# Output projection of each 256 token block from seven half products

## The chip, the cores and the metric

One core of a Trainium2 chip runs the whole program. The metric is the device time of one execution in microseconds. Its engines are TensorE (matmuls; PE in the profile, PEld for its weight loads), VectorE (DVE), ScalarE (ACT), GpSimd (POOL) and SyncE (SP, which issues most DMAs). Each works off a queue of its own in order.

## The reference

One layer of a hybrid encoder on 2048 tokens of width 1024, with 16 meta tokens ahead. After an RMSNorm one input projection feeds two mixers, causal pooling (512 channels) and latent attention (4 heads of 128). Both are gated; then

```
mix = concat([pool_out, attn_out], axis=-1) @ w_out      # 2048 x 1024 @ 1024 x 1024
h   = h + mix
out = rmsnorm(h, final_norm_g)[:, 16:]
```

All inputs and outputs are float32.

## The kernel before

The kernel keeps float32 accuracy with float16 matmuls: a value is scaled by a power of two and split in a high and a low float16 part, and a product takes three matmuls (high x high, high x low, low x high) into one float32 sum.

The first 450 us hold the token projection and the attention. What follows is a list, TAIL (line 66), of short words that the program emits in order. `w`, `a0` to `a3`, `f`, `b` load, fold, scale and split the columns of w_in; `x3` to `x7` load and split the normalised input of a block of 256 tokens; a word of two digits such as `34` is `pair(3, 4)`: for block 3, two groups of 128 columns (each 24 matmuls of 256 columns, line 633), with the windows' sums (line 648), means (653) and gates (660 to 665) on ScalarE, VectorE and GpSimd. `o0` to `o7` load a slab of 128 rows of w_out and take the maximum of its magnitude (line 685), `s` makes the scale from it (`scale_wo`), `v0` to `v7` split a slab (`split_wo`). `p0` to `p15` prepare a tile of 128 tokens for the output projection (`op_prep`: scale and split the mixers' values, lines 747 and 748, and load the residual), and `q0` to `q15` do it (`op`).

`op` of a tile makes two halves of 512 columns. Each is 8 slabs x 3 = 24 matmuls of 512 columns into one bank (line 765); VectorE then adds the scaled sum to the residual (line 767) and ScalarE squares it (769). The last tile has one half of 512 and two pieces of 256 (LASTP). Then come the norm and the store.

The order inside a queue is the compiler's: it walks the list with a model of the engines, and an engine takes the earliest word of the list whose inputs are ready in the model. So an engine's order follows TAIL loosely; TensorE's order is fixed at compile time. TensorE writes to eight banks, six of them (tag "s", NS) for the pairs and the projection. Two pools hold two buffers each for the raw loads (`raw`), taken in turn.

Of the kernel before, what the change touches and what calls it, by code (L numbers as in the profile page):

```python
# [91 lines left out]
def hymba(tc, hT, hcat, tab, w_tok, w_m, w_out, wqT, wqr, wkT, wv, pool_w,  # L92
          gains, gkv, gfin, out):
    nc = tc.nc
# [580 lines left out]

    def load_wo(k):
        if k == 0:
            cw["wor"] = cpools[1].tile([P, KT, D], F32, name="wor")
            cw["wo"] = cpools[1].tile([P, 2, KT, D], F16, name="wo")
# [1 line left out]
        wr = cw["wor"][:, k]
        nc.sync.dma_start(out=wr, in_=w_out[:, k])
        for n in range(2):
            junk = cw["pool"].tile([P, 512], F16, name=f"woa{k}_{n}", tag="wa", bufs=1)
            nc.scalar.activation(out=junk, in_=wr[:, n * 512:n * 512 + 512], func=AF.Abs, accum_out=cw["womx"][:, 2 * k + n:2 * k + n + 1])

    def scale_of(name, cols, t, up):
        nc.vector.reduce_max(out=t[:, 0:1], in_=cols, axis=AX.X)
        spread_max(nc, bank("m", name), t, 1, 1, ident, t[:, 1:2])
        power_scale(nc, t[:, 1:2], t[:, 2:3], t[:, 3:4], up)  # L690
        return t[:, 2:3], t[:, 3:4]

    def scale_wo():
# [1 line left out]
        cw["oinv"], cw["osc"] = scale_of("womx", w[:, 0:16], w[:, 16:20], WSC)

    def split_wo(k):
        wr, wo, sc = cw["wor"], cw["wo"], cw["osc"]
        a, b = slice(0, 512), slice(512, 1024)
        nc.scalar.mul(out=wo[:, 0, k, a], in_=wr[:, k, a], mul=sc)  # L700
        nc.vector.scalar_tensor_tensor(out=wo[:, 1, k, a], in0=wr[:, k, a], scalar=sc, in1=wo[:, 0, k, a], op0=ALU.mult, op1=ALU.subtract)
        nc.scalar.mul(out=wr[:, k, b], in_=wr[:, k, b], mul=sc)
        nc.scalar.copy(out=wo[:, 0, k, b], in_=wr[:, k, b])
        nc.gpsimd.tensor_tensor(out=wo[:, 1, k, b], in0=wr[:, k, b], in1=wo[:, 0, k, b], op=ALU.subtract)
# [28 lines left out]
    mhl = {}

    def op_prep(t):
        if t == 0:
            cw["mh"] = cw["pool"].tile([P, 2, 2, KT, P], F16, name="mh", tag="x0", bufs=1, padded_shape=[P, 2, 2, KT, 136])
        mh, ml = cw["mh"][:, t % 2, 0], cw["mh"][:, t % 2, 1]
        w = mmx[t // 2]
        if t % 2 == 0:  # L740
            inv, sc = scale_of(f"mmx{t}", w[:, 0:4], w[:, 4:8], WSC)
            nc.vector.tensor_scalar(out=w[:, 8:9], in0=inv, scalar1=cw["oinv"], scalar2=float(2.0 ** (-2 * WSC)), op0=ALU.mult, op1=ALU.mult)
        sc = w[:, 7:8]
        a = attn[t // 2][:, :, (t % 2) * P:(t % 2 + 1) * P]
        m = mixg[t // 2][:, :, (t % 2) * P:(t % 2 + 1) * P]
        for o, x in ((0, m), (4, a)):
            nc.scalar.mul(out=mh[:, o:o + 4], in_=x, mul=sc)
            nc.vector.scalar_tensor_tensor(out=ml[:, o:o + 4], in0=x, scalar=sc, in1=mh[:, o:o + 4], op0=ALU.mult, op1=ALU.subtract)
# [4 lines left out]
    def op(t):
        mh, ml, xr = mhl.pop(t)
        gf = cw["gf"]
        ss = cpools[1].tile([P, 6], F32, name=f"oss{t}", tag="oss", bufs=3)
        pieces = ((0, 512), (512, 512)) if t < SEQ // P - 1 else LASTP
        for hf, (c0, w) in enumerate(pieces):
            ps = bank("s", f"op{t}_{hf}")
            sl = slice(c0, c0 + w)  # L760
            i = 0
            for k in range(KT):
                wh, wl = cw["wo"][:, 0, k], cw["wo"][:, 1, k]
                for (x, y) in ((mh, wh), (mh, wl), (ml, wh)):
                    nc.tensor.matmul(ps[:, :w], lhsT=x[:, k], rhs=y[:, sl], start=i == 0, stop=i == 3 * KT - 1)  # L765
                    i += 1
            nc.vector.scalar_tensor_tensor(out=xr[:, sl], in0=ps[:, :w], scalar=mmx[t // 2][:, 8:9], in1=xr[:, sl], op0=ALU.mult, op1=ALU.add)  # L767
            sq = cw["pool"].tile([P, 512], F16, name=f"osq{t}_{hf}", tag="wa", bufs=1)
            nc.scalar.activation(out=sq[:, :w], in_=xr[:, sl], func=AF.Square, scale=1.0 / 32.0, accum_out=ss[:, hf:hf + 1])  # L769
        nc.vector.reduce_sum(out=ss[:, 4:5], in_=ss[:, 0:len(pieces)], axis=AX.X)  # L770
# [166 lines left out]
```

## Time and profile before

| | us |
|---|---|
| median of 3 runs | 890.15 (888.6 to 891.38) |
| the profiled execution | 889.79 |
| its span, first to last instruction | 888.0 |
| TensorE busy | 848.8 |
| VectorE busy | 536.8 |
| ScalarE busy | 480.6 |
| GpSimd busy | 321.3 |

The span is the profiled execution's own; 1.8 us of its time lie outside. Busy time is the union of an engine's instructions: matmuls overlap, so the sum of their durations is more than their busy time. A row of a group gives busy time and the mean of one instruction; a row of the timeline gives start, length and how many instructions are merged in it.

### The profile page before, as it was taken

How to read it: one execution, taken by the hardware profiler on the slowest of the kernel's cores; microseconds unless marked ns; L12 is line 12 of the kernel's file. 1: busy time of each engine (PE TensorE's matmuls, PEld its weight loads, DVE VectorE, ACT ScalarE, POOL GpSimd, SP SyncE). 2: the span in 40 equal slices, each digit the busy share in tenths (PEclk: the TensorE clock that was granted, in tenths of full speed). 3: DMA queues.
4: the chain of work that ended last, by engine and by line, in shares of the span. 5: the costliest groups of instructions: out<-in, count | busy, mean ns of one | idle time of the engine just before them, and what ended most of it. 6: DMA issues, size and time to landing. Idle time of an engine off the chain costs nothing. (4 is left out here: it accounts for less than half of the span.)

```text
span 888.0 us, 16286 instructions
## 1 busy us (share of the span) xinstructions
PE 848.8 (96%) x5835; PEld 684.0 (77%) x5835; DVE 536.8 (60%) x1268; ACT 480.6 (54%) x1268; POOL 321.3 (36%) x512
## 2 busy tenths in 40 slices
PE   9979989999999999898888998999999999999996
PEld 8969968889888888787877897866666666667644
DVE  6657769856757667878624578775455344435242
ACT  6656756757777667785634684854242332232321
POOL 2666642434545453645313124641141121111100
PEclk9989999999999999998999999999999999999998
DMA  8755525977798788884786112212133122111111
GB/s 287 219 170 161 163 46 100 175 145 136 131 148 150 137 153 155 168 156 130 147 180 247 48 55 76 75 26 76 48 90 107 48 72 72 48 49 48 48 40 56
DMA packets 206956, 101.80 MB, mean 115 GB/s; under 512 B 169257, under 2 KB 196363, under 8 KB 206875
## 3 DMA queue, kind: packets, MB, share of 16 engines
q1 hardware_dynamic: 187392, 93.30, 44.0%
q10 hardware_dynamic: 19483, 7.47, 3.7%
q8 instruction: 46, 0.75, 0.4%
q14 instruction: 35, 0.29, 0.1%
HBM read 55.60 MB, written 8.43 MB: 72 GB/s over the span
## 5 line engine op out<-in xcount | busy, mean ns | idle before, releaser
L633 PEld LDWEIGHTS <-w 128*128 128x128 f16 x2304 | 226.8, 99 | 36.7 <-ACT w L617 2.3
L633 PE MATMUL mp<-xx,w 128*128 128x256 f16 x2016 | 229.4, 275 | 0.6 <-DVE gt L662 0.6
L765 PE MATMUL op<-wo,mh 128*128 128x512 f16 (+1 forms) x792 | 168.1, 373 | 0.0
L765 PEld LDWEIGHTS <-mh 128*128 128x128 f16 x792 | 77.5, 98 | 85.5
L472 POOL TENSOR_TENSOR hl<-p,hl 128x512 f16<-128x512 f32 (+4 forms) x104 | 105.0, 1031 | 94.9 <-ACT hl L470 94.8
L467 ACT ACTIVATE p<-s,st 128x512 f32<-128x512 f32 (+8 forms) x168 | 99.4, 600 | 63.2 <-DVE st L452 53.0
L446 DVE TENSOR_REDUCE st<-s 128x1 f32<-128x512 f32 (+6 forms) x154 | 88.7, 589 | 19.0 <-PE s L444 17.5
L503 PE MATMUL o<-pt,vh 128*128 128x256 f16 x544 | 92.2, 274 | 2.3 <-DMA pt<-hl 2.3
L470 ACT CAST hl<-p 128x512 f16<-128x512 f32 (+6 forms) x168 | 82.5, 541 | 4.1 <-DMA pt<-hl 3.9
L769 ACT ACTIVATE osq<-xr 128x512 f16<-128x512 f32 (+1 forms) x33 | 20.4, 617 | 100.0 <-DVE xr L767 78.0
L503 PE MATMUL o<-pt,vl 128*128 128x256 f16 x272 | 74.4, 274 | 0.0
L660 ACT ACTIVATE th<-mp,whalf 128x256 f32<-128x256 f32 x64 | 30.0, 469 | 72.6 <-PE mp L633 58.7
L767 DVE SCALAR_TENSOR_TENSOR xr<-op,mmx,xr 128x512 f32<-128x512 f32 (+1 forms) x33 | 24.2, 734 | 72.4 <-PE op L765 72.4
L503 PEld LDWEIGHTS <-vh 128*128 128x128 f16 x544 | 52.1, 98 | 11.6 <-issue 2.6
L771 POOL TENSOR_SCALAR oss<-oss 128x1 f32<-128x1 f32 x16 | 3.9, 246 | 154.6 <-DVE oss L770 154.6
L472 DVE TENSOR_TENSOR hl<-p,hl 128x512 f16<-128x512 f32 (+7 forms) x64 | 50.6, 792 | 8.1 <-ACT hl L470 7.5
L440 PE MATMUL s<-klo,qh 128*128 128x512 f32 (+9 forms) x116 | 46.2, 398 | 8.5 <-ACT p L467 5.4
L573 DVE SCALAR_TENSOR_TENSOR yr<-yr,gxs,rbc 128x256 f32<-128x256 f32 (+1 forms) x64 | 35.5, 617 | 15.8 <-DMA yr<-hT_in 15.7
L441 PE MATMUL s<-klo,qh 128*128 128x512 f32 (+9 forms) x116 | 43.5, 375 | 0.0
L442 PE MATMUL s<-klo,ql 128*128 128x512 f32 (+9 forms) x116 | 43.5, 375 | 0.0
L444 PE MATMUL s<-klo,qr 128*128 128x512 f32 (+9 forms) x116 | 43.2, 373 | 0.0
L577 POOL TENSOR_TENSOR xx<-yr,xx 128x512 f16<-128x512 f32 x28 | 36.0, 1299 | 19.8 <-ACT xx L576 19.8
(229 smaller groups left out, 1756.6 us busy)
## 6 DMA issues: line engine op xcount, KB each, us to landing
xt<-hcat_in SPq DMA_DIRECT2D x16, 512.0 KB, 6.7
xr<-hcat_in SPq DMA_DIRECT2D x16, 512.0 KB, 3.8
raw<-hT_in SPq DMA_DIRECT2D x15, 512.0 KB, 5.0
out_dram<-xr SPq DMA_DIRECT2D x15, 512.0 KB, 2.7
yr<-hT_in SPq DMA_DIRECT2D x14, 512.0 KB, 3.8
wr<-w_m_in SPq DMA_DIRECT2D x12, 512.0 KB, 4.2
rb<-rd ACTq DMA_DIRECT2D x32, 128.0 KB, 4.6
wor<-w_out_in SPq DMA_DIRECT2D x8, 512.0 KB, 6.5
```

The source lines that it names most:

```text
L440: nc.tensor.matmul(ps[:, :w], lhsT=q(qh), rhs=kt[:, 0, 0, sl], start=True, stop=False)
L441: nc.tensor.matmul(ps[:, :w], lhsT=q(qh), rhs=kt[:, 1, 0, sl], start=False, stop=False)
L442: nc.tensor.matmul(ps[:, :w], lhsT=q(ql), rhs=kt[:, 0, 0, sl], start=False, stop=False)
L444: nc.tensor.matmul(ps[:, :w], lhsT=q(qr), rhs=kt[:, 1, 1, sl], start=False, stop=True)
L446: nc.vector.reduce_max(out=mx[:, bi:bi + 1], in_=ps[:, :w], axis=AX.X)
L467: nc.scalar.activation(out=pr[:, o:o + w], in_=pss[bi][:, :w], func=AF.Exp, bias=nb_, accum_out=sm[:, bi:bi + 1] if nb > 1 else tot)
L470: nc.scalar.copy(out=hl[:, 0, sl], in_=pr[:, sl])
L472: eng.tensor_tensor(out=hl[:, 1, sl], in0=pr[:, sl], in1=hl[:, 0, sl], op=ALU.subtract)
L503: nc.tensor.matmul(ps[:, :2 * P], lhsT=v, rhs=x, start=i == 0, stop=i == len(ops) - 1)
L577: nc.gpsimd.tensor_tensor(out=xl[:, k:k + 2], in0=xr[:, k - k0:k - k0 + 2], in1=xh[:, k:k + 2], op=ALU.subtract)
L633: nc.tensor.matmul(ps[:, :n - sk], lhsT=a[:, k], rhs=x[:, k, sk:n], start=e == 0, stop=e == 3 * KT - 1)
L765: nc.tensor.matmul(ps[:, :w], lhsT=x[:, k], rhs=y[:, sl], start=i == 0, stop=i == 3 * KT - 1)
```

## The change

A block of 256 tokens is a matrix of two halves of rows (its two tiles, A1. and A2.) and two halves of columns (pooling and attention, A.1 and A.2); w_out is cut in quarters in the same way. The four half products of the block, each a sum of two products of quarters, eight in all, are made from seven products of sums and differences of the quarters (Strassen's method in Winograd's form). The sums are made in float32 and then split in float16 pairs.

For w_out four sums are made for each slab pair (t1 to t4), and seven matrices are split in place of four; `split_wo(n)` works on slab pair n // 2, an even n making the sums and three of the splits, an odd n the other four. For a block, `op_prep` of the even tile makes the sums and five splits, of the odd tile two splits. `op` of the even tile makes five products (pa to pe) and of the odd tile two (pf, pg); a term that several halves share is kept over the first tile's attention values (`common`). The split tiles of a block are held once; before, those of two tiles in turn. The residual tiles of both halves of a block are in use together. w_out's buffer is cut in 32 slots, of which three hold splits of the block. The scale's exponent is 12 for 14. TAIL has w_out's loads and its scale earlier, and the first product behind pair 40.

```diff
-TAIL = """w f0 15 a1 b0 24 25 f1 00 a2 b1 10 o0 20 f2 01 a3 b2 o1 11 o2 21 f3 o3 02 b3 o4 12 o5 22 o6 03 o7 13 x3 s 23 v0
-          30 v1 x4 31 v2 v3 32 v4 33 v5 34 v6 p0 v7 35 p1 g q0 40 x5 41 p2 q1 42 p3 43 q2 44 p4 45 q3
-          p5 50 x6 q4 51 p6 52 q5 53 p7 54 q6 55 p8 60 x7 q7 61 p9 62 q8 63 p10 64 q9 65
-          p11 70 q10 71 72 p12 73 q11 74 75 p13 q12 p14 q13 p15 q14 q15"""
+TAIL = """w f0 15 a1 b0 24 o0 25 f1 o1 00 a2 o2 b1 10 o3 20 f2 o4 01 a3 b2 o5 11 o6 21 f3 o7 02 b3 s 12 22 03 v0 13 v1 x3 23 v2
+          30 v3 31 v4 x4 32 v5 33 v6 34 v7 35 p0 p1 g 40 q0 41 x5 p2 42 q1 p3 43 q2 44 p4 45 q3
+          p5 50 x6 51 q4 52 p6 q5 53 p7 54 q6 55 p8 q7 60 x7 p9 61 q8 62 p10 63 q9 64 p11 65 q10
+          70 p12 q11 p13 71 72 73 74 75 q12 p14 q13 p15 q14 q15"""
...
+    def sum_wo(name, k, x, y, op, eng, to=None):
+        to = cw["free"].pop(0) if to is None else to
+        eng.tensor_tensor(out=slot(to), in0=slot(x), in1=slot(y), op=op)
+        cw["at"][name, k] = to
+
+    def pair_wo(name, k, eng):
+        src, dst = cw["at"][name, k], cw["free"].pop(0)
+        d = slot16(dst)
+        nc.scalar.copy(out=d[:, 0], in_=slot(src))
+        eng.tensor_tensor(out=d[:, 1], in0=slot(src), in1=d[:, 0], op=ALU.subtract)
...
+        if n % 2 == 0:
+            for q in (q11, q21):
+                nc.scalar.mul(out=cw["wor"][:, q:q + 2], in_=cw["wor"][:, q:q + 2], mul=cw["osc"])
+            at["b11", k], at["b21", k], at["b22", k] = q11, q21, q22
+            sum_wo("t1", k, q12, q11, ALU.subtract, nc.vector)
+            sum_wo("t3", k, q22, q12, ALU.subtract, nc.gpsimd)
+            sum_wo("t2", k, q22, at["t1", k], ALU.subtract, nc.vector, q12)
+            sum_wo("t4", k, q21, q12, ALU.subtract, nc.gpsimd)
+            todo = (("b11", nc.vector), ("t1", nc.vector), ("t3", nc.gpsimd))
+        else:
+            todo = (("t2", nc.vector), ("b21", nc.gpsimd), ("b22", nc.vector), ("t4", nc.gpsimd))
...
+    def pair_mix(i, x, sc):
+        d = mh_slot(i).rearrange("p a (k t) -> p a k t", k=4)
+        nc.scalar.mul(out=d[:, 0], in_=x, mul=sc)
+        nc.vector.scalar_tensor_tensor(out=d[:, 1], in0=x, scalar=sc, in1=d[:, 0], op0=ALU.mult, op1=ALU.subtract)
...
+        pair_mix(0, a11, sc)
+        nc.gpsimd.tensor_tensor(out=s1, in0=a21, in1=a22, op=ALU.add)
+        pair_mix(1, a12, sc)
+        nc.gpsimd.tensor_tensor(out=a21, in0=a11, in1=a21, op=ALU.subtract)
+        nc.vector.tensor_sub(out=a11, in0=s1, in1=a11)
+        pair_mix(2, a11, sc)
+        pair_mix(3, s1, sc)
+        nc.gpsimd.tensor_tensor(out=a12, in0=a12, in1=a11, op=ALU.subtract)
+        pair_mix(4, a12, sc)
...
+        def prod(i, ps, start, c0=0, w=512):
+            x, at = mh_slot(i), cw["at"]
+            n = 0
+            for k in range(4):
+                y = slot16(at[PROD[i][1], k])
+                for u, v in ((0, 0), (0, 1), (1, 0)):
+                    nc.tensor.matmul(ps[:, :w], lhsT=x[:, u, k * P:(k + 1) * P], rhs=y[:, v, c0:c0 + w], start=start and n == 0, stop=n == 11)
+                    n += 1
...
+        if t % 2 == 0:
+            ps = run(0, "pa")
+            evict(xr, 0, ps)
+            nc.scalar.mul(out=common, in_=four(ps), mul=sc)
+            evict(xr, 0, run(1, "pb"))
+            square(xr, 0)
+            evict_common(run(2, "pc"))
+            add_common(xr, 512, nc.gpsimd)
+            ps = run(3, "pd")
+            evict(ost[t + 1], 512, ps)
+            evict(xr, 512, ps)
+            evict(xr, 512, run(4, "pe"))
+            square(xr, 512)
+        else:
+            evict_common(run(5, "pf"))
+            add_common(xr, 512, nc.gpsimd)
+            square(xr, 512)
+            add_common(xr, 0, nc.vector if last else nc.gpsimd)
+            if last:
+                nc.vector.tensor_tensor(out=xr[:, 512:], in0=xr[:, 512:], in1=gf[:, 512:], op=ALU.mult)
+            for c0, w in ((0, 256), (256, 256)) if last else ((0, 512),):
+                evict(xr, c0, run(6, "pg", c0, w), w)
+                square(xr, c0, w)
```

## Rows read from the trace of the kernel before

**Rows 1.** Windows, projection stage: stretch, length, busy time by engine, PEclk, DMA share, GB/s.

```profile
600.00:860.00 260.00, 260.00 (x1773) 173.59 (x1772) 114.84 (x239) 81.79 (x188) 44.96 (x80) 1.00 0.18 62
```

**Rows 2.** Line 765 alone: count, duration ns min/median/max, first and last start us.

```profile
L765 PE MATMUL op<-wo,mh x792: 272/379/379, 587.5 to 880.5; 128*128 128x512 f16 x186, 128*128 128x256 f16 x12
```

**Rows 3.** Timeline of TensorE, q12 to q15: start us, length us, instruction, count.

```profile
838.93 10.52 PE L765 MATMUL op<-wo,mh 128*128 128x512 f16 x48
...
849.29 0.38 PE L81 MATMUL mmx<-ident,mmx 128*128 128x128 f32 x2
...
849.51 31.30 PE L765 MATMUL op<-wo,mh 128*128 128x512 f16 x168
```

**Rows 4.** Windows ahead of the projection; busy PE, PEld, DVE, ACT, POOL.

```profile
549.00:587.50 38.50, 37.77 (x330) 33.27 (x331) 32.48 (x60) 28.24 (x58) 23.74 (x26) 0.96 0.21 59
528.00:587.50 59.50, 56.46 (x500) 49.61 (x499) 49.12 (x100) 38.13 (x81) 28.74 (x36) 0.97 0.21 59
```

**Rows 5.** Timeline of TensorE, the last pair before the first product.

```profile
582.27 5.40 PE L633 MATMUL mp<-xx,w 128*128 128x256 f16 x48 [0.63 <-DVE gt L662]
```

**Rows 6.** Groups from 549 to 587.5: count, busy us, mean ns, idle before.

```profile
L701 DVE SCALAR_TENSOR_TENSOR wo<-wor,wmx,wo 128x512 f16<-128x512 f32 x8 | 7.4, 924 | 2.1 <-ACT wo L700 2.1
L573 DVE SCALAR_TENSOR_TENSOR yr<-yr,gxs,rbc 128x256 f32<-128x256 f32 x8 | 6.2, 835 | 1.7 <-DMA yr<-hT_in 1.7
L648 DVE TENSOR_TENSOR w<-u 128x271 f32<-128x271 f32 x5 | 4.9, 970 | 1.0 <-POOL wo L704 1.0
L653 DVE SCALAR_TENSOR_TENSOR pl<-w,u 128x256 f32<-128x256 f32 x5 | 3.8, 756 | 0.1
...
L704 POOL TENSOR_TENSOR wo<-wor,wo 128x512 f16<-128x512 f32 x8 | 10.1, 1285 | 3.3 <-ACT wo L703 3.3
...
L702 ACT ACTIVATE wor<-wor,wmx 128x512 f32<-128x512 f32 x8 | 5.7, 710 | 0.0
...
L703 ACT CAST wo<-wor 128x512 f16<-128x512 f32 x8 | 4.5, 614 | 0.0
```

**Rows 7.** Timeline: four scalings of VectorE alone, and beside GpSimd.

```profile
540.24 1.67 DVE L573 SCALAR_TENSOR_TENSOR yr<-yr,gxs,rbc 128x256 f32<-128x256 f32 x4
...
571.07 2.45 POOL L704 TENSOR_TENSOR wo<-wor,wo 128x512 f16<-128x512 f32 x2
...
571.84 3.66 DVE L573 SCALAR_TENSOR_TENSOR yr<-yr,gxs,rbc 128x256 f32<-128x256 f32 x4 [1.75 <-DMA yr<-hT_in]
```

**Rows 8.** Windows around the pause that ends at 549.

```profile
546.60:549.00 2.40, 0.09 (x1) 0.00 (x0) 0.82 (x4) 2.37 (x8) 0.67 (x2) 0.96 0.00 0
549.00:551.00 2.00, 1.91 (x9) 1.50 (x10) 1.93 (x3) 2.00 (x6) 1.67 (x2) 0.50 0.00 0
551.00:553.00 2.00, 2.00 (x15) 1.55 (x14) 1.93 (x6) 1.10 (x3) 1.65 (x3) 0.70 0.00 0
```

**Rows 9.** Groups of VectorE from 600 to the end.

```profile
L767 DVE SCALAR_TENSOR_TENSOR xr<-op,mmx,xr 128x512 f32<-128x512 f32 x30 | 22.5, 750 | 68.4 <-PE op L765 68.4
...
L748 DVE SCALAR_TENSOR_TENSOR mh<-mix,mmx,mh 128x512 f16<-128x512 f32 x14 | 10.9, 778 | 19.7 <-ACT mh L747 19.7
...
L648 DVE TENSOR_TENSOR w<-u 128x271 f32<-128x271 f32 x16 | 7.0, 437 | 5.6 <-ACT u L642 5.4
L653 DVE SCALAR_TENSOR_TENSOR pl<-w,u 128x256 f32<-128x256 f32 x16 | 6.8, 423 | 0.4
...
L573 DVE SCALAR_TENSOR_TENSOR yr<-yr,gxs,rbc 128x256 f32<-128x256 f32 x16 | 6.7, 480 | 9.8 <-DMA yr<-hT_in 9.8
```

**Rows 10.** Timeline: last block's first split, the last square, eviction, gain product.

```profile
851.85 0.75 DVE L748 SCALAR_TENSOR_TENSOR mh<-mix,mmx,mh 128x512 f16<-128x512 f32 x1 [0.49 <-ACT mh L747]
...
876.53 0.63 ACT L769 ACTIVATE osq<-xr 128x512 f16<-128x512 f32 x1 [4.53 <-DVE xr L767]
...
880.85 0.48 DVE L767 SCALAR_TENSOR_TENSOR xr<-op,mmx,xr 128x256 f32<-128x256 f32 x1 [2.14 <-PE op L765]
...
882.04 0.68 DVE L777 TENSOR_TENSOR xr<-xr,gf 128x512 f32<-128x512 f32 x1
```

More of the change, by code (lines that the diff above doesn't have):

```diff
@@ L48 @@
 WSC = 14
+OSC = 12
 ORDER = (5, 6, 7, 4)
@@ L677, in load_wo @@
         if k == 0:
[L678 to L679 removed]
+            cw["wor"] = cpools[1].tile([P, 32, 512], F32, name="wor")
             cw["womx"] = wmx.rearrange("p a b c -> p (a b c)")
[L681 to L682 removed]
+            cw["free"] = list(range(16, 29))
+            cw["at"] = {}
+        wr = cw["wor"][:, 2 * k:2 * k + 2]
+        nc.sync.dma_start(out=wr, in_=w_out[:, k].rearrange("p (a n) -> p a n", a=2))
         for n in range(2):
             junk = cw["pool"].tile([P, 512], F16, name=f"woa{k}_{n}", tag="wa", bufs=1)
[L685 removed]
+            nc.scalar.activation(out=junk, in_=wr[:, n], func=AF.Abs, accum_out=cw["womx"][:, 2 * k + n:2 * k + n + 1])
     def scale_of(name, cols, t, up):
@@ L694, in scale_wo, with slot, slot16, split_wo @@
         w = cw["womx"]
[L695 to L704, printed above, removed]
+        cw["oinv"], cw["osc"] = scale_of("womx", w[:, 0:16], w[:, 16:20], OSC)
+    def slot(i):
+        return cw["wor"][:, i]
+    def slot16(i):
+        return cw["wor"][:, i].bitcast(F16).rearrange("p (a n) -> p a n", a=2)
+    def sum_wo(name, k, x, y, op, eng, to=None):
[7 more added lines that the diff above has]
+        eng.tensor_tensor(out=d[:, 1], in0=slot(src), in1=d[:, 0], op=ALU.subtract)
+        cw["free"].append(src)
+        cw["at"][name, k] = dst
+    def split_wo(n):
+        k, at = n // 2, cw["at"]
+        q11, q12, q21, q22 = 2 * k, 2 * k + 1, 2 * k + 8, 2 * k + 9
+        if n % 2 == 0:
[9 more added lines that the diff above has]
+            todo = (("t2", nc.vector), ("b21", nc.gpsimd), ("b22", nc.vector), ("t4", nc.gpsimd))
+        for name, eng in todo:
+            pair_wo(name, k, eng)
     mmx = {}
@@ L731, in pair @@
             magnitude(i, 1, attn[i])
[L733 to L748, printed above, removed]
+    ost = {}
@@ L750, in op_prep @@
         nc.sync.dma_start(out=xr, in_=hcat[META + t * P:META + (t + 1) * P, :])
-        mhl[t] = (mh, ml, xr)
-    def op(t):
-        mh, ml, xr = mhl.pop(t)
-        gf = cw["gf"]
[L756 to L770, printed above, removed]
@@ new lines, in load_res, with op_prep @@
+        ost[t] = xr
+    def op_prep(t):
+        b = t // 2
+        if t == 0:
+            cw["mh"] = cw["pool"].tile([P, 4, 2, 512], F16, name="mh", tag="x0", bufs=1, padded_shape=[P, 4, 2, 544])
+        w = mmx[b]
+        sc = w[:, 7:8]
+        a11, a21 = (mixg[b][:, :, o:o + P] for o in (0, P))
+        a12, a22 = (attn[b][:, :, o:o + P] for o in (0, P))
+        load_res(t)
+        if t % 2:
+            pair_mix(5, a21, sc)
+            pair_mix(6, a22, sc)
+            return
+        inv, sc = scale_of(f"mmx{b}", w[:, 0:4], w[:, 4:8], OSC)
+        nc.vector.tensor_scalar(out=w[:, 8:9], in0=inv, scalar1=cw["oinv"], scalar2=float(2.0 ** (-2 * OSC)), op0=ALU.mult, op1=ALU.mult)
+        s1 = slot(cw["free"][-1]).rearrange("p (k t) -> p k t", k=4)
+        pair_mix(0, a11, sc)
[7 more added lines that the diff above has]
+        pair_mix(4, a12, sc)
@@ new lines, in op, with evict, square, add_common @@
+    def op(t):
+        b = t // 2
+        last = t == SEQ // P - 1
+        ss = cpools[1].tile([P, 6], F32, name=f"oss{t}", tag="oss", bufs=3)
+        n_ss = [0]
+        def prod(i, ps, start, c0=0, w=512):
[6 more added lines that the diff above has]
+                    n += 1
+        def evict(tile_, c0, ps, w=512):
+            sl = slice(c0, c0 + w)
+            nc.vector.scalar_tensor_tensor(out=tile_[:, sl], in0=ps[:, :w], scalar=mmx[b][:, 8:9], in1=tile_[:, sl], op0=ALU.mult, op1=ALU.add)
+        def square(tile_, c0, w=512):
+            sq = cw["pool"].tile([P, 512], F16, name=f"osq{t}_{n_ss[0]}", tag="wa", bufs=1)
+            nc.scalar.activation(out=sq[:, :w], in_=tile_[:, c0:c0 + w], func=AF.Square, scale=1.0 / 32.0, accum_out=ss[:, n_ss[0]:n_ss[0] + 1])
+            n_ss[0] += 1
+        gf = cw["gf"]
+        sc = mmx[b][:, 8:9]
+        common = attn[b][:, :, 0:P]
+        four = lambda v: v.rearrange("p (k t) -> p k t", k=4)
+        def add_common(tile_, c0, eng):
+            v = four(tile_[:, c0:c0 + 512])
+            eng.tensor_tensor(out=v, in0=v, in1=common, op=ALU.add)
+        def run(i, name, c0=0, w=512):
+            ps = bank("s", f"{name}{b}_{c0}")
+            prod(i, ps, True, c0, w)
+            return ps
+        def evict_common(ps):
+            nc.vector.scalar_tensor_tensor(out=common, in0=four(ps), scalar=sc, in1=common, op0=ALU.mult, op1=ALU.add)
+        xr = ost.pop(t)
+        if t % 2 == 0:
[21 more added lines that the diff above has]
+                square(xr, c0, w)
+        nc.vector.reduce_sum(out=ss[:, 4:5], in_=ss[:, 0:n_ss[0]], axis=AX.X)
```

8 lines of the change are left out of this document (5 added, 3 removed).

## The prediction, made before the changed kernel was run

> **What bounds the kernel now.** I read the busy time by stage first, since the change lies in the last third. In the stage of the output projection TensorE is busy for 260.0 of 260.0 us at a granted clock of 1.00, with VectorE at 114.8, ScalarE at 81.8 and GpSimd at 45.0 [rows 1]. So a matmul taken out there is worth its full distance from the next one, until another engine sets the pace. That distance isn't the 379 ns of the instruction's row, which overlap with the next matmul [rows 2]. In the timeline 48 wide matmuls begin at 838.93 and TensorE's next work at 849.29: 10.36/48 = 0.216 us each [rows 3].
>
> Second, the stage ahead of the projection, in which w_out is scaled and split. The reader is to see that it is nearly full on the other engines: from 549 to 587.5 VectorE is busy 32.5 and GpSimd 23.7 of 38.5 us [rows 4], and TensorE once waits 0.63 us until VectorE frees a bank [rows 5]. Third, the very end, where no matmul hides anything [rows 10].
>
> **Removed.** A 256 token block needs 2 tiles x 2 halves x 24 = 96 wide matmuls before, and 7 products x 12 = 84 after. The last tile has one half product in narrow matmuls, 24 for 48, which the count takes as half as many wide ones. Eight blocks: 96 x 0.216 = 20.7 us. This is the gain if all else keeps up.
>
> **Added to the split of w_out.** Before, ScalarE has 16 scalings and 8 casts of 512 columns for it, VectorE 8 operations, GpSimd 8. After, ScalarE has 8 scalings of 1024 and 28 casts, VectorE 8 sums and 16 differences, GpSimd 8 and 12.
> ScalarE: 16 x 0.71 + 8 x 0.61 = 16.2 before [rows 6]. A scaling of 1024 is not in the trace; it costs between one and two of 512, and I take 1.3, near two: 8 x 1.3 + 28 x 0.61 = 27.5, so 11.3 more. ScalarE has room, 38.1 busy of 59.5 [rows 4].
> VectorE: 8 x 0.75 = 6.0 undisturbed before. A sum in f32 from SBUF has its nearest row in the gain product at the end, 0.68 [rows 10], and its upper bound in the split's 0.92 in the crowd [rows 6]. I take 0.73: 24 x 0.73 = 17.5, so 11.5 more (10 to 16).
> GpSimd: 12 more at 1.285 = 15.4 [rows 6].
>
> **How much of that is late.** Four pairs (12, 22, 03, 13) now stand behind w_out's scale, not before it. A pair is 5.2 us, 582.27 to 587.5 [rows 2, 5], so the scale can come 21 us sooner, near 528 for 549. The first product now stands behind pair 40, so it is due at 592.8 for 587.5. The window is 65 us. VectorE's load in it: 49.1 us from 528 to 587.5 before [rows 4], 11.5 from above, 1.8 for pair 40 (four operations of 0.42 to 0.48), 3.0 for the first block's preparation (four more of 0.75). Then the disturbance. Beside GpSimd four operations that take 1.67 us alone take 3.66 [rows 7]. In the crowded stage VectorE's four groups with two inputs from SBUF have means of 0.92, 0.84, 0.97 and 0.76 for 0.75, 0.48, 0.44 and 0.42 [rows 6, 9]; times their counts that is 8.6 us, 0.36 for each of GpSimd's 23.7. GpSimd's 15.4 + 3.9 (three sums for the first block) then cost VectorE 6.9. Sum 72.3 for 65: 7.3 too much. Of it some 3.7 (the preparation of products two to five) is due only while the first product runs. I take the first product 3.6 us late. Bounds: nothing, if the scale comes sooner still, and 23.5, from the second rival.
> A wait also costs clock: behind the pause of 2.3 us before 549 the next two stretches of 2 us have a granted clock of 0.50 (the lower level) and 0.70 [rows 8], so 1.0 + 0.6 = 1.6 us. I charge 1.5. That pause, the wait for w_out's scale, I leave as it is; if it goes, 3.9 are won.
>
> **Added to each block.** Preparation: 3 more scalings on ScalarE (0.71), 3 more splits (0.77) and a sum on VectorE, 3 sums on GpSimd. Eviction: 8 for 4 operations of 0.75 on VectorE [rows 9], one more on ScalarE, 3 sums on GpSimd. VectorE 3.0 + 3.0 = 6.0, GpSimd 6 x 1.29 = 7.7 per block. Seven blocks lie in the 260 us stage: VectorE 114.8 + 42 + 0.36 x 54 = 176, GpSimd 45 + 54 = 99, of the 241 that are left. Both stay under TensorE, and six banks lie between. What is queued: an eviction stands on VectorE's queue behind splits that wait for GpSimd's sums, and the next pair's gates behind it. I charge 1 us of waits for banks (0 to 10).
> The block's split tiles are held once, no longer twice. A slot is free when its own product is done, so the next block's preparation starts while the others are read. The tight place is the last block: its scale's matmul stands behind q12, and the odd tile between, q13, is 24 matmuls, 5.2 us. Before, from that matmul at 849.29 to the end of the first split at 852.60 it took 3.3 us [rows 3, 10], so it fits; with three more evictions ahead it is 1 us late. DMAs: the same number and bytes; the odd tile's residual must land a product earlier, and it is issued a pair ahead.
>
> **The end.** Behind product six the last tile has an eviction into the common term 0.75, a sum on GpSimd 1.29, a square 0.63, the gain product 0.68 on VectorE: 3.4 us without gaps [rows 6, 9, 10]. The seventh product runs beside it in two narrow halves, 24 x 0.108 = 2.6 us. VectorE reaches the last eviction 0.8 to 1.3 us late; I take 1.0. What follows, from 880.85 to 888.0, is as before [rows 10].
>
> **Sum.** -20.7 + 3.6 + 1.5 + 1.0 + 1.0 = -13.6. The profiled execution took 889.79 us (a span of 888.0 and 1.8 around it), 0.36 under the median of the three timed runs, 890.15. That gives 876.2 by the profile and 876.5 by the median. I say 876.
>
> **The rivals.**
> Nothing is late: the earlier scale gives the splits all the room they need. -20.7 + 1.0: 870. For it: ScalarE half idle, the last 3.7 us of preparation not due. Against: 72.3 for 65.
> The two engines exclude each other, and the kernel is slower. If a VectorE operation with two inputs from SBUF and one of GpSimd never ran together, the added 11.5 + 15.4 for the splits and 3.0 + 3.9 for the first block would add up to 33.8, and GpSimd's own operations lengthen by some 0.18, 20 x 0.18 = 3.6. The window has 59.5 - 49.1 = 10.4 idle on VectorE and 5.3 - 1.8 more: 13.9. The first product is 23.5 late; with clock, banks and end 27 against 20.7: 896. It decides where the first product is over 17 us late. For it: 3.66 for 1.67 [rows 7]. Against: 32.5 + 23.7 = 56 us went into 38.5 while TensorE waited 0.63 at one place.
> The Trainium skill has this as a rule (SBUF — State Buffer, § SBUF: two separate sides): the ports that the two share are an exclusive lock, and the loser stands still for the whole instruction. By that rule this rival is the forecast; the trace shows the blocking, and over the stage more overlap than the rule leaves.
> The projection stage falls behind: evictions behind GpSimd's sums hold banks for 1 us in each block, and the last block's preparation is 1 us late. 8 more than my sum: 884.
>
> **How the numbers follow.** The forecast 0.42, nothing late 0.26, the projection stage 0.18, the exclusion 0.14, of which 0.04 would end within the bound. About 0.3% (2.7 us) is what a measurement of this kernel can tell from no change. Faster 0.83, same 0.06, slower 0.11. The forecast's own bounds are 872 to 881; the range leaves out most of the exclusion and what lies well under "nothing late": 866 to 890.
>
> **What would show it.** 684 matmuls of the projection for 792, 0.216 us apart. VectorE over 90% busy and GpSimd over 70% from 528 to the first product, which starts near 596 behind 3 to 4 us in which TensorE waits for a split. In the projection stage VectorE idle ahead of its evictions until TensorE, as before. The span's end 8.5 us behind the start of the last matmul, for 7.5 now [rows 2]. Wrong if TensorE idles over 6 us ahead of the first product, if it idles over 3 us inside the projection stage, or if the matmuls' distance grows.

## The result: slower by 1.5%

| | before | after |
|---|---|---|
| median (lowest to highest), us | 889.38 (885.21 to 891.38, 4 runs) | 903.08 (895.21 to 904.61, 4 runs) |
| the profiled execution; its span, us | 889.79; 888.0 | 902.36; 900.5 |
| ratio of the medians | | 1.0154, interval 1.0119 to 1.019 |

The forecast was 876, in a range that ended at 890. Of the four executions after, the one of 895.21 had a mean granted clock of TensorE of 0.972, the others 0.965 to 0.967. The attention ahead of the change ends at another time in each execution (466 to 476 us in the profiles below), so I compare distances inside one profile from here on. Four marks serve for this: the first and the last `wmx` matmuls of eight, which belong to the maxima of w_in, the first product's first matmul, and the span's end. Stretch A lies between the first two marks, B runs to the first product, C to the end. TensorE's timeline gives them; its columns are start, length, instruction, count, and in brackets the idle time before it with what ended it. First before:

```profile
472.97 1.16 PE L81 MATMUL wmx<-ident,wmx 128*128 128x128 f32 x8 [0.61 <-DVE wr L601]
...
523.42 1.06 PE L81 MATMUL wmx<-ident,wmx 128*128 128x128 f32 x8
```

and after:

```profile
472.75 1.16 PE L81 MATMUL wmx<-ident,wmx 128*128 128x128 f32 x8 [0.61 <-DVE wr L601]
499.60 0.79 PE L81 MATMUL wmx<-ident,wmx 128*128 128x128 f32 x2 [2.40 <-ACT woa L686]
...
531.91 1.06 PE L81 MATMUL wmx<-ident,wmx 128*128 128x128 f32 x8
532.81 0.39 PE L81 MATMUL womx<-ident,wmx 128*128 128x128 f32 x2
...
565.68 3.17 PE L633 MATMUL mp<-xx,w 128*128 128x256 f16 x14 [3.61 <-DVE gt L662]
571.25 8.03 PE L633 MATMUL mp<-xx,w 128*128 128x256 f16 x58 [2.40 <-DVE gt L662]
580.35 5.40 PE L633 MATMUL mp<-xx,w 128*128 128x256 f16 x48 [1.07 <-DVE gt L662]
...
600.48 9.69 PE L633 MATMUL mp<-xx,w 128*128 128x256 f16 x72 [2.68 <-ACT u L642]
...
618.77 1.04 PE L815 MATMUL pa<-wor,mh 128*128 128x512 f16 x2 [3.14 <-ACT mh L769]
620.76 4.45 PE L815 MATMUL pa<-wor,mh 128*128 128x512 f16 x10 [0.95 <-DVE mh L770]
```

The reader is to see three things. A has grown from 50.4 to 59.2, with a wait on ScalarE for `woa`, the maxima of w_out. B has grown from 64.1 to 86.9, of which 5.2 are the pair 40 that now lies in it. Four of its waits, 8.2 us in all, are for VectorE to free a bank, where [rows 5] had one of 0.63; 3.5 us are for ScalarE to do so (L642). And the first product itself waits for its splits. The windows tell the same from the engines' side (stretch; length; busy PE, PEld, DVE, ACT, POOL; PEclk; DMA share; GB/s). B before:

```profile
523.42:587.51 64.09, 61.05 (x543) 53.81 (x541) 53.55 (x110) 40.06 (x86) 28.74 (x36) 0.97 0.21 57
```

Then after: B, the five products of the first tile, the rest up to 880, and the stretch that answers to [rows 1]:

```profile
531.91:618.77 86.86, 70.88 (x591) 59.55 (x589) 78.24 (x130) 50.81 (x99) 57.41 (x56) 0.92 0.15 42
618.77:636.56 17.79, 16.28 (x62) 6.46 (x63) 15.83 (x19) 6.57 (x13) 11.27 (x10) 0.81 0.20 59
636.56:880.00 243.44, 243.44 (x1683) 164.61 (x1681) 173.41 (x288) 95.83 (x210) 106.03 (x117) 1.00 0.19 64
...
600.00:860.00 260.00, 254.88 (x1770) 174.48 (x1770) 189.63 (x318) 108.08 (x239) 123.91 (x138) 0.98 0.19 62
```

In B TensorE fills 61.1 of 64.1 before, and VectorE 78.2 of 86.9 after: the fullest engine is another. From 636.56 on TensorE is full again, as in [rows 1].

The loss, term by term, against the kernel before: A +8.7; B +17.5 (86.86 for 64.09 + 5.24); the first tile's 60 matmuls 17.8 for 60 x 0.216 = 13.0, so +4.8; the end +2.4; the matmuls saved -20.7. Sum +12.7, which is 427.8 for 415.0 from the first mark to the end.

### The profile page after: what moved, and what is told of

Its sections match the earlier page's. It is cut to its first block, busy times and chain, and to the rows that moved or that the text cites. A ratio compares the mean times of both kernels' runs of the same rounds, so it can differ in the third digit from the quotient of the medians.

```text
span 900.5 us, 16277 instructions
## 1 busy us (share of the span) xinstructions
PE 840.2 (93%) x5727; PEld 676.2 (75%) x5727; DVE 629.2 (70%) x1349; ACT 510.4 (57%) x1312; POOL 416.4 (46%) x571
## 5 line engine op out<-in xcount | busy, mean ns | idle before, releaser
L633 PEld LDWEIGHTS <-w 128*128 128x128 f16 x2304 | 229.2, 100 | 54.7 <-issue 10.2
L633 PE MATMUL mp<-xx,w 128*128 128x256 f16 x2016 | 234.7, 278 | 11.8 <-DVE gt L662 8.2
L446 DVE TENSOR_REDUCE st<-s 128x1 f32<-128x512 f32 (+6 forms) x154 | 88.4, 588 | 18.8 <-PE s L444 17.5
L815 PEld LDWEIGHTS <-mh 128*128 128x128 f16 x384 | 38.0, 100 | 51.4 <-ACT mh L769 3.4
L824 ACT ACTIVATE osq<-xr 128x512 f16<-128x512 f32 (+1 forms) x33 | 20.3, 615 | 68.9 <-DVE xr L820 59.2
L834 POOL TENSOR_TENSOR xr<-xr,at 128x512 f32<-128x512 f32 x23 | 35.6, 1558 | 44.7 <-DVE at L842 44.7
L815 PEld LDWEIGHTS <-wor 128*128 128x128 f16 x300 | 29.4, 98 | 31.5
L573 DVE SCALAR_TENSOR_TENSOR yr<-yr,gxs,rbc 128x256 f32<-128x256 f32 (+1 forms) x64 | 40.5, 688 | 9.3 <-DMA yr<-hT_in 7.9
L755 POOL TENSOR_TENSOR at<-at,gt 128x256 f32<-128x256 f32 x32 | 25.3, 792 | 43.2 <-DVE gt L665 31.7
L444 PE MATMUL s<-klo,qr 128*128 128x512 f32 (+9 forms) x116 | 43.4, 374 | 0.0
L443 PE MATMUL s<-klo,qr 128*128 128x512 f32 (+9 forms) x116 | 43.1, 372 | 0.0
```

The source lines that it names most:

```text
L443: nc.tensor.matmul(ps[:, :w], lhsT=q(qr), rhs=kt[:, 0, 1, sl], start=False, stop=False)
L444: nc.tensor.matmul(ps[:, :w], lhsT=q(qr), rhs=kt[:, 1, 1, sl], start=False, stop=True)
L446: nc.vector.reduce_max(out=mx[:, bi:bi + 1], in_=ps[:, :w], axis=AX.X)
L633: nc.tensor.matmul(ps[:, :n - sk], lhsT=a[:, k], rhs=x[:, k, sk:n], start=e == 0, stop=e == 3 * KT - 1)
L815: nc.tensor.matmul(ps[:, :w], lhsT=x[:, u, k * P:(k + 1) * P], rhs=y[:, v, c0:c0 + w], start=start and n == 0, stop=n == 11)
```

## The experiments

All distances in one table. A row's expected B and C depend on where its list puts the first product: with 11 pairs in B, as before, the gain alone gives 64.1 and 279.8; with 12 pairs 69.3 and 274.6, with 13 74.6 and 269.3. "First tile" runs from the first product's start to the end of the fifth. The gain alone would give a total of 394.3.

| kernel | A | B (pairs) | first tile | C | total | median, us |
|---|---|---|---|---|---|---|
| before | 50.4 | 64.1 (11) | | 300.5 | 415.0 | 889.4 |
| after | 59.2 | 86.9 (12) | 17.8 | 281.7 | 427.8 | 903.1 |
| e1, new method, old list | 51.5 | 82.2 (11) | 26.4 | 295.3 | 428.9 | 900.6 |
| e2, old method, new list | 58.2 | 75.0 (12) | | 295.5 | 428.7 | 900.7 |
| e3, splits on VectorE | 59.4 | 78.8 (12) | 14.3 | 278.3 | 416.4 | 888.3 |
| e4, no low parts of w_out | 59.2 | 71.7 (12) | 18.0 | 282.0 | 413.0 | 886.7, one run |
| e8, last block's order | 55.1 | 86.7 (12) | 17.8 | 280.4 | 422.2 | 896.2, one run |
| e9, loads later | 51.5 | 86.9 (12) | 18.9 | 281.2 | 419.6 | 890.4, one run |
| e12, e9 with e3 | 51.4 | 82.2 (12) | 18.8 | 281.9 | 415.5 | 888.7 |
| e13, e12 with e8 | 50.1 | 82.3 (12) | 20.3 | 281.9 | 414.3 | 887.1 |
| e6, sums of the raw slabs | 53.0 | 73.8 (12) | 18.0 | 280.5 | 407.3 | 880.4 |
| e7, e6 and product a pair later | 52.4 | 73.8 (13) | 18.2 | 278.9 | 405.2 | 876.7 |

**List and method apart.** e1 is the changed kernel with the list of before; e2 is the kernel before with the changed list.

```diff
-TAIL = """w f0 15 a1 b0 24 o0 25 f1 o1 00 a2 o2 b1 10 o3 20 f2 o4 01 a3 b2 o5 11 o6 21 f3 o7 02 b3 s 12 22 03 v0 13 v1 x3 23 v2
...
+TAIL = """w f0 15 a1 b0 24 25 f1 00 a2 b1 10 o0 20 f2 01 a3 b2 o1 11 o2 21 f3 o3 02 b3 o4 12 o5 22 o6 03 o7 13 x3 s 23 v0
...
```

(This is e1; e2 has the same lines the other way round.)

> The changed kernel with the list TAIL of the kernel before, nothing else. Theory 'maxima': w_out's 16 maxima, earlier in the list, stand on ScalarE ahead of the maxima and splits of w_in, and put the last of w_in's four scale matmuls 8.5 us late (531.9 for 523.4). Then it is back at 523 to 524 here. Theory 'crowd' (the splits' extra work on VectorE and GpSimd is what makes the first product late): the scale of w_out is near 549 again, the splits have 20 us less, so the first product, due at 587.5, comes at 612 to 622 all the same and the time is 895 to 905. Rival 'order' (the new list alone made it late, the work fits): first product at 590 to 595, time near 875.

> The kernel before with the new list TAIL, eight half products, 8 slabs split as before. Theory 'maxima': the last scale matmul of w_in near 532, 8 us late, and the time near 897. Theory 'crowd': from there to the first product 12 pairs with at most 3 us of waits, 64 to 68 us, for 87 in the changed kernel. Rival 'order': 80 us or more here too, and time over 905.

e1 has a ratio of 1.0132 (1.01 to 1.0163), e2 of 1.013 (1.0092 to 1.0167). So each half of the change alone is about as slow as the whole. But the method's half has the saved matmuls in it: measured from what the gain alone would give, the list costs 13.7 us (428.7 for 415.0), the method 34.6 (428.9 for 394.3), both together 33.5. The losses don't add. The list, with not one split more, costs 7.7 us in A and 5.7 in B; C shrinks by 5.0, the pair that moved. The method alone leaves A almost as it was, but B is 18.1 longer and the first tile takes 26.4 for 13.0. In its list the first product stands one pair behind the last split, in the changed list two. In e1, A and the time are as expected, but the first product starts at 603.7, between the 590 to 595 of 'order' and the 612 to 622 of 'crowd'. In e2, A is as expected, but B lies between the 64 to 68 of 'crowd' and the 80 of 'order', so neither fits, and the time is over the 897. In e2 the wait in A stands where it stands after:

```profile
496.20 0.80 PE L81 MATMUL wmx<-ident,wmx 128*128 128x128 f32 x2 [2.40 <-ACT woa L685]
...
528.47 1.06 PE L81 MATMUL wmx<-ident,wmx 128*128 128x128 f32 x8
...
560.17 3.13 PE L633 MATMUL mp<-xx,w 128*128 128x256 f16 x16 [3.38 <-ACT xx L576]
565.89 32.31 PE L633 MATMUL mp<-xx,w 128*128 128x256 f16 x272 [2.59 <-DVE gt L662]
603.50 2.75 PE L765 MATMUL op<-wo,mh 128*128 128x512 f16 x12
```

**GpSimd's part on VectorE.** The same work, but the 8 sums and 12 low parts of w_out that GpSimd had are given to VectorE, the engine that is already the fullest.

```diff
-            sum_wo("t3", k, q22, q12, ALU.subtract, nc.gpsimd)
+            sum_wo("t3", k, q22, q12, ALU.subtract, nc.vector)
...
```

The sum t4 and the splits of t3, b21 and t4 are moved in the same way.

> The changed kernel with the 20 operations of w_out's splits that GpSimd did on VectorE (44 there, none on GpSimd). Theory 'exclusion' (VectorE's operations with two inputs from SBUF and GpSimd's hold each other up, so what counts is the sum of both): 20 x 1.5 of GpSimd against 20 x 0.7 more of VectorE, so the first product comes 5 to 15 us sooner than 618.8, and the time is 890 to 898. Rival 'volume' (VectorE's own count of operations is the limit): 20 x 0.7 = 14 us later, 630 or more, time near 915.

888.28 us (884.64 to 894.39, 10 runs), ratio to before 0.9991 (0.9965 to 1.0018), so about 15 faster than after, and below the 890 to 898 expected. (The profiled execution took 894.39; its attention ended late, at 476.2.) B is 8.1 shorter, within the 5 to 15 expected, and the first tile 3.5. The groups of VectorE in B (count, busy us, mean ns of one, idle before) show how an engine gets done sooner with more to do. After:

```profile
L713 DVE TENSOR_TENSOR wor<-wor 128x512 f16<-128x512 f32 x16 | 16.5, 1046 | 0.0
L573 DVE SCALAR_TENSOR_TENSOR yr<-yr,gxs,rbc 128x256 f32<-128x256 f32 x20 | 13.0, 704 | 0.0
L706 DVE TENSOR_TENSOR wor<-wor 128x512 f32<-128x512 f32 x8 | 7.5, 953 | 3.5 <-ACT wor L722 2.3 <-POOL wor L706 1.2
L751 DVE SCALAR_TENSOR_TENSOR mix<-pl,psi,gt 128x256 f32<-128x256 f32 x10 | 7.2, 716 | 0.1
...
L713 POOL TENSOR_TENSOR wor<-wor 128x512 f16<-128x512 f32 x12 | 17.2, 1442 | 4.7 <-ACT wor L712 4.7
...
L706 POOL TENSOR_TENSOR wor<-wor 128x512 f32<-128x512 f32 x8 | 13.1, 1640 | 19.0 <-ACT wor L722 11.6 <-DVE wor L713 4.1 <-DVE wor L706 3.2
```

and e3:

```profile
L713 DVE TENSOR_TENSOR wor<-wor 128x512 f16<-128x512 f32 x28 | 22.3, 818 | 0.0
L573 DVE SCALAR_TENSOR_TENSOR yr<-yr,gxs,rbc 128x256 f32<-128x256 f32 x19 | 11.3, 647 | 0.0
L706 DVE TENSOR_TENSOR wor<-wor 128x512 f32<-128x512 f32 x16 | 10.6, 685 | 1.4 <-ACT wor L722 1.2
...
L751 DVE SCALAR_TENSOR_TENSOR mix<-pl,psi,gt 128x256 f32<-128x256 f32 x8 | 3.8, 477 | 0.0
```

A sum takes 685 ns for 953, a difference 818 for 1046, a gated mean 477 for 716. VectorE has 20 more of w_out's operations in B (145 operations in all for 130), yet is busy 75.0 us in it for 78.2, and idle 3.8 for 8.6. So 3.2 of the 8.1 are busy time. The other 4.8 are waits: after, VectorE waits 1.2 us for GpSimd's sums and 3.7 for ScalarE's gates (L664), in e3 for neither. e3 shows that VectorE's operations get shorter; it doesn't part that from the hand-overs that it saves.

**The low parts left out.** The 28 differences that make the low parts of w_out aren't made, and each product reads the high part in their place; no matmul is saved.

```diff
         nc.scalar.copy(out=d[:, 0], in_=slot(src))
-        eng.tensor_tensor(out=d[:, 1], in0=slot(src), in1=d[:, 0], op=ALU.subtract)
...
-                    nc.tensor.matmul(ps[:, :w], lhsT=x[:, u, k * P:(k + 1) * P], rhs=y[:, v, c0:c0 + w], start=start and n == 0, stop=n == 11)
+                    nc.tensor.matmul(ps[:, :w], lhsT=x[:, u, k * P:(k + 1) * P], rhs=y[:, 0, c0:c0 + w], start=start and n == 0, stop=n == 11)
```

> The changed kernel without the 28 differences that make the low parts of w_out's splits (16 on VectorE, 12 on GpSimd); the products take the high part twice instead. Casts, sums and matmuls all stay. Theories 'exclusion' and 'volume' alike: 16 x 0.7 + 12 x 1.4 = 28 us less on the two, first product between 595 and 603, time 882 to 887. Rival 'chain' (the casts on ScalarE, which stands in order, or the sums' chain sets it): first product after 612, time over 895.

886.72, one run. B falls from 86.9 to 71.7, 2.4 above its bound; A and the first tile stay. With 28 of the 44 operations gone, 16 are left, as many as the splits had before the change, and with them go 15.2 of the 17.5 by which B is late, and nothing of A and of the first tile. Whether it is their number or their sharing that costs, e4 doesn't tell.

**The loads later.** `o0` to `o7` begin behind a2 and b1, as in the list of before, and are all out ahead of `s`, which keeps its place.

```diff
-TAIL = """w f0 15 a1 b0 24 o0 25 f1 o1 00 a2 o2 b1 10 o3 20 f2 o4 01 a3 b2 o5 11 o6 21 f3 o7 02 b3 s 12 22 03 v0 13 v1 x3 23 v2
+TAIL = """w f0 15 a1 b0 24 25 f1 00 a2 b1 10 o0 20 f2 01 a3 b2 o4 11 o1 21 f3 o5 02 b3 o2 o6 o3 o7 s 12 22 03 v0 13 v1 x3 23 v2
...
```

> The changed kernel with the words o0 to o7 back behind a2 and b1 (loads and maxima of w_out later in the list), the scale still ahead of pairs 12, 22 and 03. Theory 'maxima': from the first scale matmul of w_in to the last, 59.2 us in the changed kernel and 50.5 before, is 50 to 52 us here; from there to the first product stays at 85 to 90; time 893 to 897. Rival (not the maxima but the rest of the list): still 58 to 60.

890.43, one run. The timeline of TensorE has no wait for `woa` any more:

```profile
468.80 1.16 PE L81 MATMUL wmx<-ident,wmx 128*128 128x128 f32 x8 [0.61 <-DVE wr L601]
491.90 1.06 PE L81 MATMUL wmx<-ident,wmx 128*128 128x128 f32 x8
...
520.33 1.06 PE L81 MATMUL wmx<-ident,wmx 128*128 128x128 f32 x8
```

A is 51.5, 7.6 of the 8.7 are back, and B stays at 86.9 to a tenth, though w_out's scale now comes 13.2 us into it, for 0.9. The time is under the 893 to 897 expected. That settles where the wait in A comes from: the maxima of w_out had been put ahead of those of w_in on ScalarE, which takes them in order.

**The last block's order.** The odd tile's product pf is run between pc and pd of the last block, and the last sum is VectorE's.

```diff
+            if t == SEQ // P - 2:
+                evict_common(run(5, "pf"))
             ps = run(3, "pd")
...
-            evict_common(run(5, "pf"))
-            add_common(xr, 512, nc.gpsimd)
+            if not last:
+                evict_common(run(5, "pf"))
+            add_common(xr, 512, nc.vector if last else nc.gpsimd)
```

> The changed kernel with the last block's sixth product run between the third and the fourth, and the last tile's sum into its second half on VectorE instead of GpSimd. Theory 'end chain' (behind the sixth product an eviction, a sum, a square stand in a row, and the seventh product is too short to cover them): the start of the last product to the end of the span, 12.5 us in the changed kernel (887.98 to 900.5), falls to 10 to 10.8; nothing else changes. Rival (the end is set by the last two evictions and squares alone, as before): 12 to 12.5.

896.17, one run. From the start of the last product, pg, to the end it takes 11.1 us for 12.5, and not the 10 to 10.8 expected. The total is 5.6 shorter, but 4.0 of that are in A, where the edit changes nothing in the list. The windows of A, before, after and in e8, tell what it is:

```profile
472.97:523.42 50.45, 47.49 (x408) 41.69 (x409) 27.44 (x65) 34.32 (x87) 12.81 (x20) 0.97 0.34 116
...
472.75:531.91 59.16, 52.17 (x408) 44.59 (x409) 28.43 (x67) 38.79 (x99) 12.75 (x20) 0.88 0.32 112
...
471.90:527.04 55.14, 48.04 (x408) 41.80 (x409) 28.74 (x68) 38.90 (x99) 12.88 (x20) 0.97 0.34 120
```

The 408 matmuls are the same, and TensorE is idle for 7.0 and 7.1 us; but after it is busy 4.1 us longer, at a granted clock of 0.88 for 0.97 (a mean between its two levels, 0.5 or 1.2 GHz and 1.0 or 2.4 GHz). Both have the wait of 2.4 us for `woa`; behind it a pair of `wmx` matmuls takes 0.79 us after and 0.49 in e8. Why the clock fell there in one execution and not in the other, the runs don't show. So of A's 8.7 after, 4.0 are waits and 4.7 a slower TensorE (52.17 for 47.49). I count the 1.4 for e8's edit. The end after, to be held against [rows 10], shows what they were:

```profile
887.98 2.78 PE L815 MATMUL pg<-wor 128*128 128x256 f16 x24
...
889.15 1.28 DVE L872 SCALAR_TENSOR_TENSOR xr<-xr,oss,gf 128x1024 f32<-128x1024 f32 x1 [0.99 <-POOL oss L870]
890.35 0.74 DVE L842 SCALAR_TENSOR_TENSOR at<-pf,mmx,at 128x512 f32<-128x512 f32 x1
...
891.17 1.77 POOL L834 TENSOR_TENSOR xr<-xr,at 128x512 f32<-128x512 f32 x1 [2.06 <-DVE at L842]
...
892.97 0.63 ACT L824 ACTIVATE osq<-xr 128x512 f16<-128x512 f32 x1 [5.01 <-POOL xr L834]
```

The sixth product's eviction (L842) stands behind the norm of the even tile, 1.28 us on VectorE, and GpSimd's sum takes 1.77 beside VectorE's.

**Both causes at once.** e12 joins e9's list and e3's engines, e13 adds e8's order. They ask whether the losses add up.

> The changed kernel with two edits at once: o0 to o7 back behind w_in's maxima (alone: 8.1 us less from w_in's maxima to the end) and the sums and low parts of w_out on VectorE instead of GpSimd (alone: 11.4 us less). If the two losses are separate, the distance from the first wmx matmul to the end is 427.8 - 8.1 - 11.4 = 408 us and the time 883 to 884, 0.993 of the kernel before. Rival: both are one loss, since whatever the first delays the second makes good (VectorE's 82 us of work between the scale and the first product are the limit either way): then the distance stays near 416 and the time near 889, no change.

> The kernel with the loads later and the splits on VectorE, and with the last block's sixth product run ahead of its fourth, so that a narrow sum fewer stands behind the last matmul. From the start of the last product to the end it takes 11.1 us for 12.5, so 1.4 us less than without this edit: 882 if the losses are separate. Rival: the last block's preparation is late by this order (the odd tile's splits are due sooner), and the time is the same or longer.

e12: 888.69 (886.27 to 891.02, 10 runs), ratio 1.0012 (0.9991 to 1.0033). The expectation of 883 to 884 was wrong and its rival right: the total is 415.5, and only 0.9 less than with e3 alone. Against e3, A is 8.0 shorter, but B is 3.4 and the first tile 4.5 longer. In e12 the scale of w_out comes later, seen from the start of B:

```profile
522.94 1.06 PE L81 MATMUL wmx<-ident,wmx 128*128 128x128 f32 x8
536.36 0.46 PE L81 MATMUL womx<-ident,wmx 128*128 128x128 f32 x2 [2.31 <-DVE wmx L689]
```

That is 13.4 us into B, for 0.9 after and in e3. No split may begin before it, so the splits have the other 68.8. In B VectorE is busy 78.0 of 82.2 (95%):

```profile
522.94:605.16 82.22, 68.06 (x594) 58.82 (x592) 78.03 (x153) 53.28 (x109) 30.91 (x36) 0.97 0.19 56
```

Early loads delay w_in; late loads, beside e3's engines, delay the first product and its tile by as much, and the 8 us are moved, not won. In e9, with the engines of the changed kernel, the same list won 8.1, its B no longer for it. That the squeeze of the splits is what costs in e12 is argued, not shown. e13: 887.13 (881.82 to 891.01, 10 runs), ratio 0.9985 (0.996 to 1.001); from pg to the end 11.0 us for 12.5 in e12, as expected, but the time misses its 882 and is within the interval of no change.

**Sums that don't wait for the scale.** A power of two can be applied behind a sum as well as ahead of it. In e6 the sums are made from the raw slabs, ahead of `s`, and the scale goes into the splits. All of it is on VectorE and ScalarE; e9's loads and e8's order are kept. So e13 is its neighbour. The four sums of each slab pair become words of their own, d0 to d3.

```diff
-            for q in (q11, q21):
-                nc.scalar.mul(out=cw["wor"][:, q:q + 2], in_=cw["wor"][:, q:q + 2], mul=cw["osc"])
...
-        nc.scalar.copy(out=d[:, 0], in_=slot(src))
-        eng.tensor_tensor(out=d[:, 1], in0=slot(src), in1=d[:, 0], op=ALU.subtract)
+        nc.scalar.mul(out=d[:, 0], in_=slot(src), mul=cw["osc"])
+        nc.vector.scalar_tensor_tensor(out=d[:, 1], in0=slot(src), scalar=cw["osc"], in1=d[:, 0], op0=ALU.mult, op1=ALU.subtract)
```

e7 puts the first products one pair later (`41` ahead of `q0`, and so on to block 5).

> Seven products as in the changed kernel, with four edits: the 16 sums of w_out are made from the raw slabs (words d0 to d3, ahead of the scale), each split is a scaling on ScalarE and one operation on VectorE that scales and subtracts (as before the change), nothing of it on GpSimd; o0 to o7 later in the list; the last block's order as in e8. GpSimd loses 20 x 1.5 us, VectorE has 44 operations for 24, of which 16 no longer wait for the scale; ScalarE loses 8 scalings of 1.13. Theories 'exclusion' and 'maxima': first wmx to last 50 to 53, from there to the first product 65 to 74 for 86.9, time 866 to 876. Rival 'volume': first product as late as before, time over 888.

> As e6, with every product one pair later in the list up to block 2. If the splits are still late in e6, this wins 2 to 5 us over it (5.2 us more for 2.7 us more work on VectorE); if e6 has TensorE busy up to the first product, the same time as e6 within 2 us.

e6: 880.36 (878.33 to 881.27), ratio 0.9894 (0.9868 to 0.9919), total 7.0 less than e13. A and B are where they were expected, the time is over its 866 to 876. e7: 876.67 (875.36 to 879.94), ratio 0.985 (0.9823 to 0.9878). It is faster than both kernels, and wins the 2 to 5 us expected over e6 (3.7 by the medians, 2.1 by the totals). e6 has several edits at once, and no run parts them. The B of e7, to be held against that of e12 above, though it has a pair more:

```profile
525.17:598.97 73.80, 70.44 (x637) 62.37 (x637) 67.88 (x137) 50.69 (x108) 33.04 (x38) 1.00 0.17 49
```

VectorE has 10 us less in B. Most of it is that 12 of the 16 sums lie in A (2.7 us of sums in B for 11.6), where VectorE is busy 35.5 of 52.4 (27.4 of 50.4 before). TensorE's is again the fuller row. What e7 still lacks to 394.3 is 10.9: A 2.0, the first tile 5.3, the end 1.1 (8.3 us behind TensorE's last matmul for 7.2), and some 3.3 of waits later in C; B is 0.8 under its bound.

## Why the prediction was wrong, step by step

**Removed: right.** The profile has 108 + 6 x 96 = 684 matmuls of the projection, and from pf to pg in the last block, 885.39 to 887.98, twelve take 2.59 us, 0.216 each. The 20.7 came.

**How much of that is late: the step that failed.** It had "I take the first product 3.6 us late". B is 17.5 late, and A, which the step took as given, 8.7. The term that weighs most, and that the sum had at nothing, is the time for which VectorE stands idle in its full window.
In B I had VectorE's work too high and its disturbance too low. Taking each group's count in B by the mean that it has undisturbed (0.43 us for L648, 0.47 for L573, 0.41 for L653 and L665, 0.47 for the gated mean, 0.68 for the sums and differences, 0.75 for the splits of before), the work is 58.9 us for 47.6 before: 11.3 more, where I had 16.3. What the operations took beyond that, by their means, is 28.1 for 12.1: 16.0 more, where I had 6.9. I had 0.36 us of disturbance for each us of GpSimd, from four groups. Over all of B it is 12.1/28.7 = 0.42 before, 28.1/57.4 = 0.49 after, and between 0.36 (e6, e7) and 0.50 in the kernels of the table. And GpSimd's busy time doubled, 57.4 for 28.7, where I had 19.3 more: its differences take 1.44 us and its sums 1.64, for 1.285 [rows 6].
The means of neighbours overlap by up to 0.08 us (the rows of e12 at the end show it), so work and disturbance sum to more than the busy time. In busy time VectorE has 24.7 more in B (78.2 for 53.5). I had 23.2, the 11.5, 1.8, 3.0 and 6.9 together: the two errors nearly cancel, which is luck. Of the 23.2 I left 3.7 for later, so 19.5 should have fallen in B.
The second error was to spend the whole window. VectorE was idle for 8.6 of 86.9 (10.5 of 64.1 before): 3.7 in wait for ScalarE's gates (L664), 3.5 for ScalarE's scalings and GpSimd's sums [L706 above], and ScalarE waits 11.2 us for VectorE's differences. With that B's account closes: the first product comes 13.9 later in it than the 3.6 of the forecast, 5.2 by busy time (24.7 for 19.5) and 8.6 by idle time. The forecast's own sign, TensorE idle for over 6 us ahead of the first product, came with 16.0 (86.9 less 70.9). The third was to let "some 3.7 (the preparation of products two to five)" run beside the first product. TensorE waits for it: the first tile takes 17.8 for 13.0. The granted clock, too, was lower where TensorE waited: 0.81 in the first tile and 0.92 in B, for 0.97 in B before. I charged 1.5 us for it. In A alone it is 4.7 (the windows under e8), and in the first tile TensorE is busy 16.3, where that of e3, at 1.00, has 13.3. In B it is busy 4.6 longer than before with one pair more (70.88 for 61.05 + 5.24), but VectorE is the fuller engine there, and what that costs isn't shown.
In A I had looked at what the scale gains by coming sooner ("21 us sooner"), and not at what its eight loads pass on ScalarE. From the first mark, the pause for w_out's scale ended at 76.0 us before (549.0 in [rows 8]); after, the scale's matmul is at 60.1, 16 sooner, where the forecast's 528 is 55.0. A paid 8.7 for it, waits and clock together. The prediction said of moved steps only what they win.

**Added to each block: right.** From 636.56 on TensorE is busy 243.4 of 243.4 at a granted clock of 1.00. VectorE has 189.6 and GpSimd 123.9 in the 260 us of [rows 1] (I had 176 and 99), and this hides under TensorE. The rival in which the projection falls behind didn't come.

**The end: too small.** It costs 2.4 and not 1.0, and the span ends 10.0 us behind the last matmul's start for 7.5 [rows 2], with 8.5 forecast. I had left out the even tile's norm ahead of the sixth product's eviction, and had priced GpSimd's sum alone.

**The rivals.** The exclusion decides "where the first product is over 17 us late"; B is 17.5 late, just past it, and 5.7 of that e2 has without a split more. That VectorE's operations get shorter when GpSimd has less to do is shown by e3, which takes back 8.1 of the 17.5. In e3's B VectorE is still busy 75.0 of 78.8, and e3 doesn't part sharing from the mere number of operations there. The rival's price of 896 lacked A, and had the whole of GpSimd's time as lost where half is. The argument I set against it, that 56 us of both went into 38.5 while TensorE waited only 0.63, showed that there was still slack; the slack was then spent. In that stage before the change 0.42 of GpSimd's time was already paid by VectorE, and one row by form for all of B would have told it.

**What stays open.** e2 has 5.7 in B without a split more. Its two long waits are 3.4 for ScalarE's cast of a block's input (L576) and 2.6 for VectorE to free a bank (L662), but I didn't follow them back. Nor did I try what would bring the first tile from 18 to 13; in e7 VectorE is busy 17.3 of 18.2 there. Why the clock fell in A after and not in e8, behind the same wait, is open.

## What to carry to other kernels

Where work is added to a stage, sum it for each engine with the disturbance over all its groups in that stage, then add an allowance for the idle time of its hand-overs (in B VectorE's was 3.8 to 13.9 us, so that is a guess until it is run); if the sum passes the length, that engine is likely the new bound, and what is "due later" may be waited for there too. A step that is moved forward in a list passes others on each in-order queue that it uses: look for what stands behind it there, and count a clock that may fall behind the wait. If the bound is an engine that shares something with a neighbour, giving it the neighbour's work can be faster, and work that needn't wait for a scale belongs ahead of it.
